# A decoder trunk on one Trainium2 core: the residual turned so that tokens lie on the partitions

## The chip, the core and the metric

The kernel runs on one core of a Trainium2 chip. The time is what the device takes for one execution, in microseconds, as the median of several runs. TensorE (PE, with its weight loads as PEld) multiplies; VectorE (DVE), ScalarE (ACT) and GpSimd (POOL) work element by element, and DMA queues issued by SyncE (SP) bring data in and out. On the chip, SBUF holds 128 partitions; products are summed in PSUM banks of 128 x 512 f32.

## What is computed

Two layers, each with a SwiGLU FFN, a mixer and a second FFN, on 512 tokens of width 1024. Each is wrapped in two RMS norms, over the 1024 features of a token:

```python
def _rmsnorm(x, g):
    return x * lax.rsqrt(jnp.mean(x * x, axis=-1, keepdims=True) + RMS_EPS) * g
def _swiglu(h, w_gate, w_up, w_down):            # 1024 -> 2816 -> 1024
    return (jax.nn.silu(h @ w_gate) * (h @ w_up)) @ w_down
...
for l in range(DEPTH):                            # 2 layers, g = norm_g[l]
    f = _swiglu(_rmsnorm(x, g[0]), ...)
    x = x + 0.5 * _rmsnorm(f, g[1])
    m = _mixer(_rmsnorm(x, g[2]), ...)
    x = x + _rmsnorm(m, g[3])
    f = _swiglu(_rmsnorm(x, g[4]), ...)
    x = x + 0.5 * _rmsnorm(f, g[5])
```

The mixer projects h into queries, keys and values of 8 heads of 64, a gated causal convolution of width 3 over 256 channels, and trailing means over 2, 4, 8 and 16 tokens with a small map over 256 more; the three results, 1024 channels, go through an output projection. The attention is a stick-breaking one: the weight of key s for query t is sigmoid(z) times the product of 1 - sigmoid(z) over the keys between them. The kernel takes that product as a sum of logarithms over the keys.

## The kernel before

**Precision.** Each f32 operand is split into a high part (a cast to f32r) and a low part (the rest). A product is three matmuls: high by high, high by low, low by high.

**Weights.** They come as units of 128 x 1024 (512 KB), each by one DMA. ACT makes the high part `wh` (L167), DVE the low part `wl` (L173). Raw units, parts and most larger tiles share a pool of 31 slots, and loads and splits run ahead as far as slots are free.

**The residual** `x` lies with features on the partitions: 8 blocks of 128 features by 512 tokens. A product's stationary operand is the weight, its moving operand 512 tokens of h.

**FFN.** The 22 blocks of 128 hidden channels come in chunks of 6, 8 and 8. For each block gate and up are accumulated over 8 blocks of features, in two PSUM banks `psz`. `evac` (L465 to L474) multiplies both by `rbs`, the broadcast norm factor, takes Silu on ACT, multiplies, and writes hid as high (ACT) and low part (POOL). After a chunk the down projection runs, one unit for each of the 8 feature blocks of the output, and DVE adds it to `f` (L512).

**Boundaries.** The last chunk's down projection (and likewise the mixer's output projection) is split: the last 7 units (5 for the mixer) run in token halves of 256 columns, so that the norm of the first half can start while PE works on the second. Squares are taken by ACT (L365) and summed over feature blocks by POOL and DVE into `ss` (L376). `rstd` sums `ss` over the partitions with one-column products (`pss<-mat,ss`), POOL takes the power -0.5 (L387), DVE puts the factors on a diagonal and PE broadcasts it over the partitions (`pss<-pH,none_`). `boundary` (L415 to L446) then multiplies f, adds to x, and makes the parts of h for two feature blocks at a time. h isn't normalised: the factor is applied where products leave PSUM.

**The order on PE** is that of the program: `mm` (L270) chains every matmul to the one ahead and adds to a running estimate of time. Side work (statistics, a head's sums and values) is a generator which names the delay after which it wants its next turn; `poll`, called between the products of a unit, starts what is due. `need` forces side work up to a flag.

**Attention.** A head's keys lie on the partitions and its queries along the free axis, in three tiles (384, 384 and 512 wide). `scores` makes logits and the logarithm `t` of 1 - sigmoid in parts `pH`, `pL` (L577, L581); `sums` adds the later keys inside a block by a triangular matrix `ntri` and those of later blocks by a matrix of minus ones, `none_`. Blocks needed together are added up first into a tile `later` by POOL (L622 to L624), which gets parts of its own. The projections of the next heads, the convolution and the pooling run between the heads' steps. Each eviction there multiplies by `rbs`; most additions of the pooling run on POOL.

## Time and profile before

| | us |
|---|---|
| median of 3 runs (2010.01 to 2014.77) | 2010.83 |
| the profiled execution | 2010.89 |
| its span on the core | 2009.1 |
| PE busy | 1928.6 (96%) |
| PE weight loads busy | 1658.7 (83%) |
| DVE busy | 1038.1 (52%) |
| ACT busy | 769.6 (38%) |
| POOL busy | 384.0 (19%) |

The profile is one execution, recorded by the hardware. Each instruction has a start, a length and, where it waited, the instruction that released it. Matmuls are pipelined, so the length of a single one is longer than its share of the time; the distance from start to start tells what it costs. A group of records written x2 is two in a row. The granted clock is the share of its full speed that TensorE got: 1.00 is 2.4 GHz, and a stretch partly at 1.2 GHz lies between .50 and 1.00. Stages of the first layer: first FFN to about 380 us, mixer to about 612, second FFN to about 1000; the second layer repeats them about 995 us later.

### The profile page before, as it was taken

Reading aid. Unit: us, or ns where it says so; the run is one execution under the profiler, and the core shown is the slowest. Engines: PE = TensorE matmul, PEld = TensorE weight load, DVE = VectorE, ACT = ScalarE, POOL = GpSimd, SP = SyncE. Lnnn points to the kernel's source line nnn. Section 1 sums busy time; section 2 is a strip of 40 time slices with the busy share of each in tenths; the row PEclk is TensorE's granted clock in tenths of the full one; section 3 lists DMA queues with packets and bytes.
Section 4 is the critical chain, followed back from the end, with each engine's and each line's share of the span. In section 5 each row is a group of like instructions: output and inputs, shape, how many; then the busy total and the mean of one; then the engine's idle time right before and its main releaser. Section 6 shows DMA issues by size and latency. Waiting matters only on the chain.

```text
span 2009.1 us, 25060 instructions
## 1 busy us (share of the span) xinstructions
PE 1928.6 (96%) x9908; PEld 1658.7 (83%) x9908; DVE 1038.1 (52%) x1487; ACT 769.6 (38%) x1223; POOL 384.0 (19%) x397
## 2 busy tenths in 40 slices
PE   8999999998989999999989999999998989999997
PEld 7888888887778888888988888888877888888887
DVE  7334434678857434434573343448687483343343
ACT  5223223456654332222443221335566442322232
POOL 3101011421315101001430010115131251010012
PEclk8999999999989999999999999999998989999998
DMA  5232323221221232232222323222211112323321
GB/s 198 78 124 74 115 92 108 74 63 43 65 72 43 84 126 84 85 115 89 93 72 94 105 84 115 86 93 74 65 62 53 63 63 75 125 84 97 113 74 43
DMA packets 52102, 174.19 MB, mean 87 GB/s; under 512 B 5520, under 2 KB 9872, under 8 KB 51984
## 3 DMA queue, kind: packets, MB, share of 16 engines
q1 hardware_dynamic: 51984, 172.59, 26.7%
q8 instruction: 78, 1.28, 0.3%
q14 instruction: 40, 0.33, 0.1%
HBM read 170.47 MB, written 2.10 MB: 86 GB/s over the span
## 4 chain that ended last, share of the span: by engine, by line
PE 83%; DVE 10%; ACT 3%; issue 2%; POOL 1%; DMA 0%; SPq 0%; DVEq 0%; ACTq 0%; POOLq 0%
PE psz L270 50%; PE psd L270 32%; DVE h L415 2%; DVE pH L439 2%; DVE pL L581 1%; DVE pH L577 1%; DVE wl L173 1%; PE pss L270 1%; ACT wh L167 1%; POOL x L442 1%; ACT h L414 1%; DVE t L614 1%; ACT t L347 0%; DVE ss L376 0%; ACT pL L365 0%
## 5 line engine op out<-in xcount | busy, mean ns | idle before, releaser
L270 PE MATMUL psz<-h,wh 128*128 128x512 f32 (+1 forms) x3168 | 906.6, 372 | 6.6 <-DVE t L465 3.0
L270 PEld LDWEIGHTS psz<-h,wh 128*128 128x128 f32 x3168 | 586.9, 194 | 105.0 <-issue 4.6
L270 PE MATMUL psz<-h,wl 128*128 128x512 f32 (+1 forms) x1584 | 587.3, 371 | 1.2 <-DVE wl L173 1.2
L173 DVE TENSOR_TENSOR wl<-raw,wh 128x1024 fp32r<-128x1024 f32 (+1 forms) x328 | 411.3, 1269 | 328.7 <-ACT wh L167 163.2
L270 PE MATMUL psd<-hid,wh 128*128 128x512 f32 (+1 forms) x1856 | 457.8, 338 | 0.0
L167 ACT CAST wh<-raw 128x1024 fp32r<-128x1024 f32 (+1 forms) x326 | 325.2, 1025 | 171.0 <-DVE wl L173 88.8
L270 PEld LDWEIGHTS psd<-hid,wh 128*128 128x128 f32 x1856 | 320.3, 190 | 37.7
L270 PEld LDWEIGHTS psz<-h,wl 128*128 128x128 f32 x1584 | 307.0, 194 | 49.3 <-DVE wl L173 1.7
L474 POOL TENSOR_TENSOR hid<-t,hid 128x512 fp32r<-128x512 f32 (+1 forms) x99 | 118.3, 1195 | 1112.1 <-ACT hid L473 1112.1
L270 PE MATMUL psd<-hid,wl 128*128 128x512 f32 (+1 forms) x928 | 313.9, 338 | 0.0
L466 DVE TENSOR_TENSOR t<-psz,rb 128x512 f32<-128x512 f32 (+1 forms) x99 | 62.4, 630 | 348.5 <-PE psz L270 348.5
L473 ACT CAST hid<-t 128x512 fp32r<-128x512 f32 (+1 forms) x99 | 56.6, 573 | 433.9 <-DVE t L468 433.8
L347 ACT ACTIVATE t<-t 128x512 f32<-128x512 f32 (+2 forms) x195 | 106.8, 571 | 247.1 <-DVE t L465 246.2
L270 PEld LDWEIGHTS psd<-hid,wl 128*128 128x128 f32 x928 | 176.2, 190 | 18.6
L270 PE MATMUL psd<-h,wh 128*128 128x512 f32 (+1 forms) x576 | 167.3, 377 | 0.0
L270 PEld LDWEIGHTS psd<-h,wh 128*128 128x128 f32 x576 | 106.3, 195 | 18.9 <-issue 1.0
L376 POOL TENSOR_TENSOR ss<-ss,pL 128x256 f32<-128x256 f32 x112 | 94.8, 851 | 101.4 <-ACT pL L365 96.9
L270 PE MATMUL psd<-h,wl 128*128 128x512 f32 (+1 forms) x288 | 107.3, 372 | 0.0
L465 DVE TENSOR_TENSOR t<-psz,rb 128x512 f32<-128x512 f32 (+1 forms) x99 | 61.7, 624 | 69.3 <-PE psz L270 68.7
L270 PE MATMUL psd<-mix,wh 128*128 128x256 f32 (+1 forms) x416 | 90.8, 317 | 0.1
L512 DVE TENSOR_TENSOR f<-f,psd 128x256 f32<-128x256 f32 (+1 forms) x92 | 47.6, 521 | 63.3 <-PE psd L270 63.3
L581 DVE TENSOR_TENSOR pL<-t,pH 128x384 fp32r<-128x384 f32 (+1 forms) x112 | 72.1, 664 | 12.2 <-ACT pH L579 9.9
(111 smaller groups left out, 1618.9 us busy)
## 6 DMA issues: line engine op xcount, KB each, us to landing
raw<-in_w_dram SPq DMA_DIRECT2D x296, 512.0 KB, 3.5
raw<-in_w_dram SPq DMA_DIRECT2D x32, 384.0 KB, 3.0
out_dram<-x SPq DMA_DIRECT2D x8, 256.0 KB, 2.8
x<-in_xt_dram SPq DMA_DIRECT2D x4, 256.0 KB, 5.5
x<-in_xt_dram SPq DMA_DIRECT2D x2, 512.0 KB, 9.3
mat<-in_mats_dram SPq DMA_DIRECT2D x1, 384.0 KB, 10.0
mat<-in_mats_dram SPq DMA_DIRECT2D x1, 128.0 KB, 8.5
cst<-in_consts_dram SPq DMA_DIRECT2D x1, 73.0 KB, 2.0
```

The costliest lines, as they stand in the source:

```text
L167: nc.scalar.copy(h[:, :n], raw[:, :n])
L173: nc.vector.tensor_tensor(lo[:, :n], raw[:, :n], f32(h[:, :n]), op=ALU.subtract)
L270: ins = nc.tensor.matmul(dst, w, r, start=start, stop=stop, skip_group_check=True)
L347: ins = nc.scalar.activation(out_, in_, f_, **kw)
L376: eng.tensor_tensor(ss[hf], ss[hf], qq, op=ALU.add)
L415: nc.vector.scalar_tensor_tensor(hL[k][:, ts], x[:, k, ts], g, f32(hH[k][:, ts]), op0=ALU.mult, op1=ALU.subtract)
L465: nc.vector.tensor_tensor(g[:, :n], pg[:, ts], rbs[:, ts], op=ALU.mult)
L466: nc.vector.tensor_tensor(u[:, :n], pu[:, ts], rbs[:, ts], op=ALU.mult)
L473: nc.scalar.copy(hid[0][:, ts], u[:, :n])
L474: nc.gpsimd.tensor_tensor(hid[1][:, ts], u[:, :n], f32(hid[0][:, ts]), op=ALU.subtract)
L512: nc.vector.tensor_tensor(f[:, n0, ts], f[:, n0, ts], ps[:, ts], op=ALU.add)
L581: eng.tensor_tensor(dstL, src, f32(dstH), op=ALU.subtract)
```

## The change

The residual is laid out as 4 blocks of 128 tokens by 1024 features.

- Down and output projections have the tokens of hid or of the mixer's result as the stationary operand (128 tokens) and the weights as the moving one (512 output features). A unit holds two blocks of input channels by half of the output features. The chunks are 8, 8 and 6. In the first two `stream` runs over both halves of the features with four banks; in the last, `by_tokens` finishes one token block after the other. The mixer's output projection has a part before the last head is done (`OUT_A`) and one behind it (`OUT_B`).
- Norms run along the free axis: ACT squares a block with a sum (`accum_out`), POOL takes the power of one column, DVE multiplies 1024 columns by factor and gain at once. Gains come as tiles of 128 x 1024 by DMA.
- h is normalised, then turned: 8 PE transposes of 128 x 128 in f32 for each token block into two banks, ACT casts the high part and DVE subtracts the low one. The turn is side work, due 13 us after the block's norm is issued. h has a place of its own, the pool has 28 slots, and `psz` has 5 banks in place of 4.
- `rbs`, the statistics and broadcast products, `later` and most of POOL's work are gone. Evictions read PSUM directly, the sums take more products with `none_`, and hid's low part and the pooling's additions are DVE's.
- At the start x comes block by block with an identity and the first gain, and h is made by the same norm and turn.

The core of the diff:

```diff
--- before.py
+++ after.py
-CHUNKS = (6, 8, 8)
+CHUNKS = (8, 8, 6)
...
-SLOTS = 31
+SLOTS = 28
...
+WARM = 24
+URGENT = 0
+
+OUT_A = ((4, 6), (7,))
+OUT_B = ((5, 0), (1, 2), (3,))
...
+D_TURN = 13
...
+                for dh in range(2):
+                    for g in _pairs(range(k0, k0 + n)):
+                        out.append(("down", l, half, (g, dh), len(g) * DH))
...
+    hHs = cpool.tile([P, KB, T], F32R, name="hh")
+    hLs = cpool.tile([P, KB, T], F32R, name="hl")
...
+        g = flat(kept("g", F32))
+        nc.sync.dma_start(out=g, in_=gains[l * 6 + i])
+        return g
...
+    def turn(dst, src):
+        ins = nc.tensor.transpose(dst, src, ident)
+        if line["last"] is not None:
+            after(ins, line["last"], "order")
+        line["last"] = ins
+        line["now"] += 0.1
...
+    def root(ms):
         nc.gpsimd.tensor_tensor(r, ms, expo, op=ALU.pow)
...
-        for i, v in enumerate((r, rest)):
-            for b in range(2):
-                nc.vector.tensor_scalar(dg[:, i, b * P:(b + 1) * P], ident, v[:, b:b + 1], -factor,
-                                        op0=ALU.mult, op1=ALU.mult)
-        yield D_BC if post else D_BC_PRE
-        ps = bank("s", 1)
-        for i in range(2):
-            mm(ps[:, :HALF], none_, dg[:, i, :], i == 0, i == 1)
-        return r, ps[:, :HALF]
...
+    def prenorm(key, tb, g, buf, free):
+
+        ss, ms = small(), small()
+        nc.scalar.activation(buf, x[:, tb, :], AF.Square, scale=D ** -0.5, accum_out=ss[:, 0:1])
+        nc.vector.tensor_scalar(ms[:, 0:1], ss[:, 0:1], EPS, None, op0=ALU.add)
+        r = root(ms[:, 0:1])
+        nc.vector.scalar_tensor_tensor(buf, x[:, tb, :], r, g, op0=ALU.mult, op1=ALU.mult)
+
+        def turned():
+            for q in range(2):
+                ps = bank()
+                for i in range(4):
+                    turn(ps[:, i * P:(i + 1) * P], buf[:, (4 * q + i) * P:(4 * q + i + 1) * P])
+                pv = ps.rearrange("p (a b) -> p a b", a=4)
+                dst = (slice(None), slice(4 * q, 4 * q + 4), tok(tb))
+                nc.scalar.copy(hHs[dst], pv)
+                nc.vector.tensor_tensor(hLs[dst], pv, f32(hHs[dst]), op=ALU.subtract)
+            done((key, "h", tb))
+            free()
+            return
+            yield
+
+        side(turned(), D_TURN)
...
+        def store(self, tb, dh, ps, f):
+
+            s = slice(dh * DH, (dh + 1) * DH)
+            if dh == 0:
+                self.ss[tb] = small()
+            nc.vector.tensor_tensor(f[:, s], f[:, s], ps, op=ALU.add)
+            nc.scalar.activation(tmp(), f[:, s], AF.Square, scale=self.scale,
+                                 accum_out=self.ss[tb][:, dh:dh + 1])
+            if dh == 1:
+                self.finish(tb, f)
+
+        def finish(self, tb, f):
+            ss, ms = self.ss.pop(tb), small()
+            nc.vector.scalar_tensor_tensor(ms[:, 0:1], ss[:, 0:1], self.eps, ss[:, 1:2], op0=ALU.add, op1=ALU.add)
+            r = root(ms[:, 0:1])
+            if self.pre is None:
+                for dh in range(2):
+                    s = slice(dh * DH, (dh + 1) * DH)
+                    nc.vector.scalar_tensor_tensor(f[:, s], f[:, s], r, self.post[:, s], op0=ALU.mult, op1=ALU.mult)
+                    nc.vector.tensor_tensor(x[:, tb, s], x[:, tb, s], f[:, s], op=ALU.add)
+                    nc.sync.dma_start(out=out[:, tb, s], in_=x[:, tb, s])
+                return
+            nc.vector.scalar_tensor_tensor(f, f, r, self.post, op0=ALU.mult, op1=ALU.mult)
+            nc.vector.tensor_tensor(x[:, tb, :], x[:, tb, :], f, op=ALU.add)
+            prenorm(self.key, tb, self.g, f, self.free)
...
+    def token_mms(ps, tb, src, blocks, w, dh_first, dh_last):
+        wH, wL = w
+        for i, b in enumerate(blocks):
+            poll()
+            sH, sL = src[b]
+            cs = slice(i * DH, (i + 1) * DH)
+            a, z = dh_first and i == 0, dh_last and i == len(blocks) - 1
+            mm(ps, sH[:, tok(tb)], wH[:, cs], a, False)
+            mm(ps, sH[:, tok(tb)], wL[:, cs], False, False)
+            mm(ps, sL[:, tok(tb)], wH[:, cs], False, z)
+
+    def stream(groups, src, store):
+
+        for dh in range(2):
+            pss = [bank("z") for _ in range(TBS)]
+            for gi, blocks in enumerate(groups):
+                w = take()
+                for tb in range(TBS):
+                    token_mms(pss[tb], tb, src, blocks, w, gi == 0, gi == len(groups) - 1)
+                    if gi == len(groups) - 1:
+                        store(tb, dh, pss[tb])
+                retire()
...
+    def by_tokens(groups, src, store):
+
+        ws = {}
+        for tb in range(TBS):
+            for dh in range(2):
+                ps = bank("z")
+                for gi, blocks in enumerate(groups):
+                    if tb == 0:
+                        ws[dh, gi] = take()
+                    token_mms(ps, tb, src, blocks, ws[dh, gi], gi == 0, gi == len(groups) - 1)
+                    if tb == TBS - 1:
+                        retire()
+                store(tb, dh, ps)
...
-            nc.vector.tensor_tensor(g[:, :n], pg[:, ts], rbs[:, ts], op=ALU.mult)
-            nc.vector.tensor_tensor(u[:, :n], pu[:, ts], rbs[:, ts], op=ALU.mult)
-            fn(g[:, :n], g[:, :n], AF.Silu)
-            nc.vector.tensor_tensor(u[:, :n], g[:, :n], u[:, :n], op=ALU.mult)
...
-            nc.scalar.copy(hid[0][:, ts], u[:, :n])
-            nc.gpsimd.tensor_tensor(hid[1][:, ts], u[:, :n], f32(hid[0][:, ts]), op=ALU.subtract)
...
+            fn(g, pg, AF.Silu)
+            nc.vector.tensor_tensor(u, g, pu, op=ALU.mult)
+            nc.scalar.copy(t[:, 0, :], u)
+            nc.vector.tensor_tensor(t[:, 1, :], u, f32(t[:, 0, :]), op=ALU.subtract)
+            return t[:, 0, :], t[:, 1, :]
...
+                    for tb in (2 * hf, 2 * hf + 1):
+                        need((n_, "h", tb))
...
-                            retire(2)
-                        when((key, "r", hf), lambda a=(pg, pu, HS[hf], hd): evac(*a))
...
-                project_out(f, hidH, hidL, n, store, finish, TAIL_F)
...
+                by_tokens(groups, src, lambda tb, dh, ps: bd.store(tb, dh, ps, f[tb]))
...
-            dense_out(range(KB), hidH, hidL, n, store)
...
+            stream(groups, src, store)
...
-                    s = tmp()
-                    eng = nc.gpsimd
-                    eng.tensor_copy(s[:, 256:384], ts[0][:, :P])
-                    eng.tensor_tensor(s[:, 384:], ts[0][:, P:256], ts[0][:, 256:384], op=ALU.add)
-                    eng.tensor_tensor(s[:, :256], s[:, 256:], t[:, P:384], op=ALU.add)
-                    self.later = self.parts(s, T, "later")
...
-                for to, src, c0, w in ((P, self.sp[0], 256, P),) if ti == 0 else (
-                        (P, self.later, 256, 256),) if ti == 1 else (
-                        (P, self.sp[1], 0, P), (256, self.later, 0, 256)):
-                    for part in src:
+                for to, src, c0, w in (((P, 0, 256, P),), ((P, 0, 0, 256), (256, 0, 256, P)),
+                                       ((P, 1, 0, 384), (256, 0, 0, 256), (384, 0, 256, P)))[ti]:
+                    for part in self.sp[src]:
                         mm(z[:, to:to + w], none_, part[:, c0:c0 + w], False, True)
...
-        def query_out(p, factor, ps):
-            t = tmp()
-            nc.vector.scalar_tensor_tensor(t, ps, factor, rbs, op0=ALU.mult, op1=ALU.mult)
...
+                    nc.scalar.activation(high[r, e, :], ps[r, :], AF.Identity, scale=factor)
...
-            nc.vector.tensor_tensor(t, ps, rbs, op=ALU.mult)
-            nc.gpsimd.tensor_tensor(u, u, t, op=ALU.mult)
+            nc.vector.tensor_tensor(u, u, ps, op=ALU.mult)
...
-                nc.gpsimd.tensor_tensor(s2[rows, w:], s[rows, w:], s[rows, :T - w], op=ALU.add)
...
+                nc.vector.tensor_tensor(s2[rows, 2 * w - 1:], s[rows, 2 * w - 1:], s[rows, w - 1:T + PAD - w], op=ALU.add)
...
-        project_out(f, [mix(i)[0] for i in blocks], [mix(i)[1] for i in blocks], KB, store, finish, TAIL_M,
-                    early=EARLY, flag=(key, "mix"))
...
+            s = slice(dh * DH, (dh + 1) * DH)
+            nc.scalar.copy(f[tb][:, s], ps)
...
+        by_halves(OUT_A, mixed, store)
...
+        need((key, "mix"))
...
+        bd = Boundary(key, l, i, pre)
+        by_tokens(OUT_B, mixed, lambda tb, dh, ps: bd.store(tb, dh, ps, f[tb]))
...
+    nc.sync.dma_start(out=x[:, 0, :], in_=xt[:, 0, :])
+    nc.sync.dma_start(out=ident, in_=mats[:, M_ID:M_ID + P])
+    slots["reserve"] += 1
+    g0 = gain(0, 0)
+    nc.sync.dma_start(out=x[:, 1, :], in_=xt[:, 1, :])
+    for i in range(2):
+        load(i)
+    for tb in range(2, TBS):
+        nc.sync.dma_start(out=x[:, tb, :], in_=xt[:, tb, :])
```

What moves on DVE is shown at three places. The first is the second head of the first mixer. Before, in the order of DVE (`t` is the logarithm, `later`'s parts are pH_3526 and pL_3527, tile 3's are pH_3539 and pL_3540, qk and q are the next query):

```order
L577 CAST pH_3526<-t_3522 128x512
L614 SCALAR_TENSOR_TENSOR t_3534<-psz_3530,t_3534 128x512
L719 SCALAR_TENSOR_TENSOR t_3582<-psd_3455,rb_226 128x512
L581 TENSOR_TENSOR pL_3527<-t_3522,pH_3526 128x512
L581 TENSOR_TENSOR mix_3567<-t_3564,mix_3567 64x512
L577 CAST pH_3539<-t_3534 128x512
L173 TENSOR_TENSOR wl_3577<-raw_3413,wh_3576 128x1024
L732 TENSOR_TENSOR qk_3584<-t_3582,q_3585 64x512
L581 TENSOR_TENSOR pL_3540<-t_3534,pH_3539 128x512
```

After, at the same head (the third tile is t_3140 with pH_3145 and pL_3146):

```order
L509 TENSOR_TENSOR pL_3120<-t_3114,pH_3119 128x384
L541 SCALAR_TENSOR_TENSOR t_3140<-psz_3136,t_3140 128x512
L506 CAST pH_3132<-t_3127 128x384
L586 TENSOR_TENSOR t_3170<-psz_3161,t_3170 64x512
L506 CAST pH_3145<-t_3140 128x512
L509 TENSOR_TENSOR pL_3133<-t_3127,pH_3132 128x384
L509 TENSOR_TENSOR pL_3146<-t_3140,pH_3145 128x512
L509 TENSOR_TENSOR mix_3173<-t_3170,mix_3173 64x512
L156 TENSOR_TENSOR wl_3183<-raw_2884,wh_3182 128x1024
```

The parts of `later`, the eviction with `rb`, a weight split and a query's part no longer stand between the third tile's logarithm and its low part.

The second place is the boundary behind the first mixer. Before, DVE multiplies f (`m`) by the broadcast factor, adds to x, and writes low parts of h for feature blocks:

```order
L439 TENSOR_TENSOR pH_5041<-m_4619,rbf_5038 128x512
L439 TENSOR_TENSOR pH_5077<-m_4619,rbf_5038 128x512
L439 TENSOR_TENSOR pH_5111<-m_4619,rbf_5038 128x512
L439 TENSOR_TENSOR pH_5156<-m_4619,rbf_5038 128x512
L442 TENSOR_TENSOR x<-x,pH_5156 128x2x256
L415 SCALAR_TENSOR_TENSOR h_5044<-x,cst,h_5044 128x256
L415 SCALAR_TENSOR_TENSOR h_5047<-x,cst,h_5047 128x256
L376 TENSOR_TENSOR ss_4646<-ss_4646,pL_5072 128x256
L415 SCALAR_TENSOR_TENSOR h_5080<-x,cst,h_5080 128x256
L415 SCALAR_TENSOR_TENSOR h_5083<-x,cst,h_5083 128x256
```

After, `f_4196`, `f_4208`, `f_4270` and `f_4294` are the four token blocks; L357 adds a half of the features, L374 and L375 are the norm behind and the residual, L321 the norm ahead, L331 the low part of turned h:

```order
L331 TENSOR_TENSOR hl<-psd_4529,hh 128x4x128
L331 TENSOR_TENSOR hl<-psd_4536,hh 128x4x128
L357 TENSOR_TENSOR f_4294<-f_4294,psz_4525 128x512
L156 TENSOR_TENSOR wl_4559<-raw_4362,wh_4558 128x1024
L374 SCALAR_TENSOR_TENSOR f_4270<-f_4270,ss_4514,g_4365 128x1024
L156 TENSOR_TENSOR wl_4568<-raw_4550,wh_4567 128x1024
L156 TENSOR_TENSOR wl_4585<-raw_4562,wh_4584 128x1024
L375 TENSOR_TENSOR x<-x,f_4270 128x1024
L357 TENSOR_TENSOR f_4294<-f_4294,psz_4577 128x512
L331 TENSOR_TENSOR hl<-psd_4602,hh 128x4x128
L331 TENSOR_TENSOR hl<-psd_4609,hh 128x4x128
```

The low part of block 1 (psd_4602) stands behind the last block's second addition, which needs the last product of the projection, and behind four weight splits, three of them shown.

The third place is the start. Before, DVE writes low parts of h for feature blocks (L415) as they come, with the first weight's split between them:

```order
L415 SCALAR_TENSOR_TENSOR h_104<-x,cst,h_104 128x256
L415 SCALAR_TENSOR_TENSOR h_107<-x,cst,h_107 128x256
L165 CAST wh_116<-raw_72 128x1024
L415 SCALAR_TENSOR_TENSOR h_110<-x,cst,h_110 128x256
L173 TENSOR_TENSOR wl_117<-raw_72,wh_116 128x1024
L415 SCALAR_TENSOR_TENSOR h_113<-x,cst,h_113 128x256
L415 SCALAR_TENSOR_TENSOR h_122<-x,cst,h_122 128x256
L415 SCALAR_TENSOR_TENSOR h_125<-x,cst,h_125 128x256
```

After, block 0's norm (f_119), two weight splits, then block 1's (ss_141, f_139):

```order
L319 TENSOR_SCALAR ss_121<-ss_120 128x1
L321 SCALAR_TENSOR_TENSOR f_119<-x,ss_124,g_108 128x1024
L156 TENSOR_TENSOR wl_128<-raw_111,wh_127 128x1024
L156 TENSOR_TENSOR wl_134<-raw_113,wh_133 128x1024
L319 TENSOR_SCALAR ss_141<-ss_140 128x1
L331 TENSOR_TENSOR hl<-psd_193,hh 128x4x128
L321 SCALAR_TENSOR_TENSOR f_139<-x,ss_144,g_108 128x1024
L331 TENSOR_TENSOR hl<-psd_200,hh 128x4x128
```

Both splits stand ahead of block 1's norm, and the first low parts of h behind block 0's turn.

## Rows read from the trace of the kernel before

**Rows 1.** stretches: length, busy us (count) of PE, PEld, DVE, ACT, POOL; clock, DMA, GB/s

```profile
0.00:50.00 50.00, 42.77 (x247) 37.23 (x248) 37.48 (x65) 25.87 (x44) 18.99 (x26) 0.86 0.55 198
50.00:360.00 310.00, 310.00 (x1439) 259.88 (x1439) 120.91 (x133) 91.23 (x119) 30.63 (x26) 1.00 0.30 96
372.00:420.00 48.00, 44.52 (x256) 39.02 (x255) 41.83 (x74) 24.00 (x46) 27.65 (x25) 0.93 0.23 77
420.00:587.00 167.00, 148.19 (x697) 124.05 (x697) 129.99 (x199) 107.98 (x188) 34.69 (x48) 0.92 0.20 64
612.00:662.00 50.00, 44.40 (x314) 43.49 (x313) 40.42 (x76) 23.39 (x49) 28.30 (x27) 0.86 0.16 53
...
996.00:1050.00 54.00, 48.97 (x368) 47.72 (x367) 47.19 (x87) 28.37 (x54) 26.93 (x25) 0.94 0.29 95
...
1984.00:2009.00 25.00, 13.24 (x103) 12.48 (x101) 13.37 (x27) 4.64 (x10) 8.04 (x7) 0.79 0.26 85
```

**Rows 2.** waits of PE, whole span: us in total, times, longest

```profile
PE pss L270 <- DVE ss L376: 21.8, 9, 3.0
PE psz L270 <- DVE pL L581: 21.5, 16, 1.8
PE psz L270 <- DVE pH L577: 10.6, 8, 3.9
```

**Rows 3.** groups by shape on PE: count, busy us, mean ns, idle before

```profile
L270 PE MATMUL psd<-hid,wh 128*128 128x256 f32 x896 | 162.0, 284 | 0.0
...
L270 PE MATMUL psd<-mix,wh 128*128 128x256 f32 x320 | 58.2, 284 | 0.1
...
L270 PE MATMUL pss<-mat,ss 128*128 128x1 f32 x96 | 16.5, 275 | 21.8 <-DVE ss L376 21.8
...
L270 PE MATMUL pss<-pH,none__80 128*128 128x256 f32 x48 | 11.2, 306 | 2.4 <-DVE rl L392 1.7 <-DVE rb L420 0.5 <-DVE pH L395 0.2
```

**Rows 4.** timeline of PE, first FFN's tail: start, length, operation, idle before

```profile
366.69 0.40 PE L270 MATMUL psd<-hid,wh 128*128 128x256 f32 x2
...
367.05 0.50 PE L270 MATMUL pss<-mat,ss 128*128 128x1 f32 x4
367.41 0.48 PE L270 MATMUL psd<-hid,wh 128*128 128x256 f32 x2
```

**Rows 5.** timeline of PE, a pooling map among projections

```profile
496.86 0.61 PE L270 MATMUL psd<-h,wh 128*128 128x512 f32 x2
...
497.54 1.02 PE L270 MATMUL psd<-c,mat 128*128 128x512 f32 x2
...
498.87 0.40 PE L270 MATMUL psd<-h,wl 128*128 128x512 f32 x1
```

**Rows 6.** timeline of DVE and PE, second head of the first mixer

```profile
451.19 0.67 DVE L581 TENSOR_TENSOR pL<-t,pH 128x512 fp32r<-128x512 f32 x1
...
452.73 1.20 DVE L173 TENSOR_TENSOR wl<-raw,wh 128x1024 fp32r<-128x1024 f32 x1
...
453.87 0.67 DVE L732 TENSOR_TENSOR qk<-t,q 64x512 fp32r<-64x512 f32 x1
...
454.47 0.67 DVE L581 TENSOR_TENSOR pL<-t,pH 128x512 fp32r<-128x512 f32 x1
...
455.19 0.50 PE L270 MATMUL psz<-pL,ntri 128*128 128x512 f32 x1 [1.84 <-DVE pL L581]
```

**Rows 7.** groups by shape on DVE and POOL

```profile
L173 DVE TENSOR_TENSOR wl<-raw,wh 128x1024 fp32r<-128x1024 f32 x296 | 375.1, 1283 | 297.7 <-ACT wh L167 144.6 <-PE psd L270 93.8 <-issue 57.9
...
L387 POOL TENSOR_TENSOR r<-ms,expo 128x2 f32<-128x2 f32 x24 | 28.5, 1187 | 81.3 <-DVE ms L385 75.4 <-DVE rl L392 5.9
...
L512 DVE TENSOR_TENSOR f<-f,psd 128x512 f32<-128x512 f32 x36 | 24.2, 680 | 0.0
```

**Rows 8.** timeline of PE: the first product on data, and the last product

```profile
7.53 0.48 PE L270 MATMUL psz<-h,wh 128*128 128x256 f32 x2 [1.59 <-ACT h L414]
...
1995.31 0.28 PE L270 MATMUL psd<-hid,wl 128*128 128x256 f32 x1
```

625 lines of the change are left out of this document (218 added, 407 removed).

## The prediction

> **What bounds the kernel now.** I read the busy times by stretch first. Between two stages TensorE works without a gap and at the full clock: 310.00 us busy of 310 at a granted clock of 1.00 [rows 1]. There the time is the number of products and nothing else, so a stretch that loses time shows as idle TensorE or as a lower clock. I take the loss of a stretch as its length less PE's busy time, plus its length times one less the clock. That gives 6.9 us for 372–420 (first FFN to mixer), 18.8 + 13.4 = 32.2 for the attention (420–587), 5.6 + 7.0 = 12.6 for mixer to second FFN (612–662), 5.0 + 3.2 = 8.3 for FFN to FFN (996–1050) and about 14 for the end [rows 1]. The second layer's stretches are the same within a microsecond. At the start 247 products of mostly 256 columns, about .12 us each (below), fill 30 of 50 us: 20 are lost. Two attentions, two boundaries before them, two behind them, one between layers, start and end: 146 us in all, seven parts in a hundred. The view of waits says for what: statistics products wait 21.8 us for DVE's sums of squares, and attention's sums wait 21.5 and 10.6 us for the low and high parts that DVE writes [rows 2]. So two things set the time: how many products there are, and how soon DVE gets to what PE wants next.
>
> **Products: the token halves.** The tails of the down and output projections run in token halves, 256 columns wide: 896 products with high weights of hid, hence 448 with low ones, and 320 + 160 of mix [rows 3]. Three of them take .36 us (366.69 to 367.05), .12 each [rows 4]; three of 512 columns take .68 (496.86 to 497.54), .227 each [rows 5]. A pair of halves so costs 13 ns more than one whole. Of the 1824 halves 912 pairs go; the projections of the first queries give another 96 and the wider head of the first FFN takes 48 back: 960 x 13.3 ns = **-12.8**. The 512-column products with tokens standing and weights moving are the same work as before otherwise, and I give them the same price.
>
> **Products: statistics.** 96 records of one column and 48 broadcasts of 256 go [rows 3]. Four of the first take .36 us (367.05 to 367.41), .09 each [rows 4]: 8.6; the second .12 each: 5.8. Together **-14.4**.
>
> **Products: `later`.** Without the pre-added sums every head needs two more products of 128 columns and two of 384. On the line through .12 for 256 and .227 for 512 these are .067 and .173: .48 a head, 16 heads, **+7.7**.
>
> **Products: transposes.** 192 blocks of 128 x 128 in f32 (six norms, four token blocks, eight each). No row shows one. The lower bound is a weight load with a one-column product, .09 [rows 4]. The upper one is an ordinary f32 product: between 497.54 and 498.87 lie one of 512 columns and two ordinary ones, 1.33 - .45 = .88 us, so .22 for 128 columns [rows 5]. I take .12, what a 256-column product costs, since it is near the lower row in form (one pass, a new weight each time): **+23**, bounds 17 to 42. All lie on PE's path, except where PE would have waited anyway. The Trainium skill, page TensorE: Matmul & The Clock Gate, Part 4: PE-mode transpose, speaks against the change here: about 275 ns for such a block inside a kernel, and the full clock not engaging for them. By that the transposes would be 53 us, and the sum 30 later. In this trace one-column products, each with a weight load of its own, come every 90 ns [rows 4], so I don't follow it.
>
> Products together: -12.8 - 14.4 + 7.7 + 23 = **+3.5**. PE's work is almost unchanged; the gain has to come from the waits.
>
> **Attention.** In the order of DVE the second head's last high part (453 us) is followed by a weight split, the query's low part and only then the low part that PE waits for: `pL` of `later` runs at 451.19, the split at 452.73, the query at 453.87, the wanted `pL` at 454.47, and PE starts at 455.19 after 1.84 us [rows 6]. The change takes from each mixer's DVE eight low parts of `later` (.67), eight evictions of queries and eight of convolution and pooling (.68): 16.3 us. It adds four multiplications and six pooling additions that POOL did, and two halves of subtractions: 12 x .68 = 8.2. So DVE, 130 us busy of 167 [rows 1], has 8 less, and nothing but the head's own work stands between its high and low parts. With these prices I followed DVE's queue head by head: waits of 1.7 at the second head, 3.5 at the third (pooling additions ahead of it), .8 at the fourth, 4 at the sixth (splits and convolution), 2 behind the last: 12 in place of 18.8. The half-clock loss falls with them, 13.4 to 8.6. That is -11.6 per mixer, **-23.2**; bounds 0 (the waits only move) and -23 per mixer (two thirds of the loss gone).
>
> **Boundaries.** Here the work changes its engine. For each token block DVE now does two additions to f (.68), three passes over 1024 columns (the price of a split, 1.28) and two low parts of h (.68): 6.6 us, with two powers on POOL (1.19 each) in between [rows 7]. Behind the mixer PE has 5 x 3 x 8 products = 27.2 us and 16 transposes to hide it. Up to the low part of block 1, which the first half of the next FFN needs, DVE's order holds 8 additions, 8 long passes, 4 splits, 4 low parts and 5 short ones (put at .16): 24.3 us, beginning 3.4 us into PE's run. If DVE waits for the first four norms, 2.2 us each (ACT's squares, power, hand-overs; an estimate from the power's 1.19), that is 36.5, while PE is through at 29.1: a wait of 7.4, which with some 5 us of lower clock is about the 12.6 of before: **0**, +-4 each. If the norms hide, only the last transposes, cast and subtraction are late, about 2.5. Behind an FFN PE has 6 x 3 x 8 products, 32.7 us: DVE at 36.5 against 34.6 leaves about 2 of wait with some 4 to 5 us of lower clock, 6.8 in place of 8.3 between layers, **-1.5**. Before the mixer the values take one block after another, 24 products (5.4 us) each; by the same queue PE waits about 3.5 at the third block, in place of a loss of 6.9 with its clock: **0**, +-3 each.
>
> **Start.** The first product on data stands at 7.53 us now [rows 8]. Afterwards two token blocks, an identity and a gain must land, and DVE has two weight splits queued ahead of block 1's norm, so PE begins at about 20, but then finds all it needs: 23 lost in place of 20, **+3** (-2 to +8). **End.** From the last product at 1995.31 [rows 8] to the end it takes 13.8 us: addition, squares, statistics, power, diagonals, broadcast, four multiplications, four additions, stores. Diagonals and broadcast go, and one block of 512 columns remains: addition, squares, power, two passes, a store: 9.5, **-4.3**.
>
> **Hidden.** The FFN's low part of hid moves from POOL to DVE, but two multiplications by the norm go there. DVE is busy 120.91 of 310 us [rows 1]; were this cover gone, every one of 88 hidden blocks would show up to .68 us. The gains add 6 MB of loads against a DMA share of .30 [rows 1].
>
> **Sum.** 3.5 - 23.2 - 1.5 + 3 - 4.3 = -22.5. The span of 2009.1 becomes 1986.6. The profiled run took 2010.89, 1.8 beyond its span, and the median of the runs is 2010.83: **1988 us**.
>
> **Rivals.** *More:* attention's waits and the lower clock almost vanish (-23 a mixer instead of -11.6) and the transposes cost .09 (-6): 1988 - 23 - 6 = 1959. For it: PE's waits there are all for DVE parts that stood behind others. Against: DVE stays over 70% busy there. *Nothing in attention:* the pooling additions and splits stand where `later` did, and PE waits as long: 1988 + 23 = 2011. For it: the splits are unchanged, ACT's chain of a head too. *Transposes as plain f32 products*, .22: +19, 2007; against it is the one-pass form, for it that every ordinary f32 product in the trace takes two records. (The Trainium skill's 275 ns would give 2018 for the same case.) *Slower:* DVE's chain of a boundary doesn't overlap with PE. Its place is the five boundaries; if each token block waits for the one ahead (addition to low part: 2 x .68 + 3 x 1.28 + 2 x .68 + 2 powers with hand-overs, about 11 us, four in a row 44) against 29 to 34 us of PE, each boundary loses 10 to 15 beyond its present loss: +50, 2038. It outweighs the gain from about 5 us per boundary on. Against it: the order interleaves two blocks.
>
> **How the numbers follow.** Forecast .57, with a range of its own of 1972 to 2003; more .12; nothing in attention .13; transposes .08; slower .10. A measurement here tells .3%, 6 us, from no change, so below 2004.8 is faster: the forecast less .02, all of the first rival, a quarter of the second and a third of the third: .73. Slower (above 2016.9): the last rival and a quarter of the second: .13. Between: .14. The range takes in half of the first rival, and leaves out most of the last: 1958 to 2022.
>
> **What would show it.** Right: transposes in rows of eight some .12 apart; PE busy for more than 153 of attention's 167 us, no wait of 2 us behind a split; the boundary behind the mixer with one wait of 2 to 7 us for DVE's h; a first product on data near 20 us; under 10 us behind the last. Wrong: transposes .2 or more apart; long PE waits for `f` or `hl` at each boundary; or weight splits that come late in the steady stretches, where PE has no idle time to hide them.

## The result

The changed kernel takes 1954.29 us (median of 4 runs, 1952.35 to 1954.8) against 2010.62 of the kernel before on the same chip: a ratio of 0.9714, with a 95% interval of 0.9697 to 0.9731. That is 56 us less, where 22.5 were forecast, and 4 us under the range of 1958 to 2022. The profiled execution took 1954.8 with a span of 1953.0.

| | before | after |
|---|---|---|
| span, us | 2009.1 | 1953.0 |
| PE busy | 96% | 98% |
| DVE busy, us | 1038.1 | 856.9 |
| POOL busy, us | 384.0 | 40.9 |

The stretches of the profile after, with the columns of [rows 1]: first the undisturbed part of the first FFN, then its boundary to the mixer, attention, the boundary to the second FFN, the one between the layers, and the second layer's attention.

```profile
58.00:357.00 299.00, 299.00 (x1295) 242.75 (x1294) 95.49 (x99) 82.45 (x101) 0.00 (x0) 1.00 0.28 95
357.00:418.00 61.00, 59.76 (x278) 49.05 (x277) 42.36 (x53) 27.39 (x47) 5.43 (x10) 1.00 0.30 102
418.00:566.00 148.00, 142.77 (x710) 119.50 (x708) 99.47 (x173) 98.30 (x183) 3.12 (x6) 1.00 0.12 42
566.00:650.00 84.00, 80.25 (x490) 72.51 (x490) 49.85 (x60) 38.12 (x63) 6.43 (x8) 0.94 0.37 132
...
972.00:1022.00 50.00, 48.93 (x369) 46.34 (x368) 32.47 (x40) 24.40 (x39) 4.72 (x5) 1.00 0.42 144
...
1382.00:1529.00 147.00, 142.65 (x706) 119.30 (x705) 99.59 (x173) 97.72 (x183) 3.33 (x7) 1.00 0.13 44
```

By the same measure as in the prediction, attention now loses 5.2 us, all of it idle time at a clock of 1.00, in place of 32.2 [rows 1]; the second layer's loses 4.4. The first of these ends at a lucky place: ahead of the last head's values PE waits 2.1 us, and the lower clock behind that wait begins where the stretch ends. The wait in the timeline of PE, and the four us behind the stretch:

```profile
564.16 0.50 PE L223 MATMUL psz<-pH,v 128*128 128x512 f32 x1 [2.12 <-ACT pH L508]
```

```profile
566.00:570.00 4.00, 4.00 (x13) 3.13 (x13) 1.61 (x2) 3.01 (x5) 0.00 (x0) 0.57 0.39 135
```

These 1.7 us belong to attention, which then loses 6.9: 25 less than before in the first layer and 28 less in the second, some 26.5 a mixer. The boundary ahead of the mixer loses 1.2 instead of 6.9, the one between layers 1.1 instead of 8.3, the one behind the mixer 3.8 idle and 5.0 by the clock, 8.8 instead of 12.6 (7.1 without those 1.7). The undisturbed stretch has PE busy for 299.00 of 299 us at 1.00, so DVE's new work is hidden there. The waits of PE over the whole span, which answer to [rows 2]:

```profile
PE psd L265 <- DVE f L321: 6.7, 3, 5.8
PE psz L223 <- DVE hl L331: 6.2, 2, 3.2
PE psz L223 <- DVE pL L509: 5.6, 10, 1.0
...
PE psz L223 <- ACT pH L508: 3.4, 2, 2.1
```

The three rows of [rows 2] summed to 54 us. The sums of a head now wait 5.6 us in all for their low parts, and the largest single wait, 5.8 us, is the one for block 1's norm at the start. The next rows are the timeline of PE, in order: the first product on data, eight transposes among the products of the first output projection and the products behind them, and the kernel's last product.

```profile
18.34 0.58 PE L223 MATMUL psz<-hh,wh 128*128 128x256 f32 x1
...
599.66 1.03 PE L265 MATMUL psd<-mat,f 128*128 128x128 f32 x8
600.45 0.48 PE L223 MATMUL psz<-wh,mix 128*128 128x512 f32 x1
600.76 0.39 PE L223 MATMUL psz<-wl,mix 128*128 128x512 f32 x1
601.00 0.62 PE L223 MATMUL psz<-wh,mix 128*128 128x512 f32 x2
...
1944.55 0.39 PE L223 MATMUL psz<-wh,hid 128*128 128x512 f32 x1
```

From the first of the eight transposes at 599.66 to the third product behind them at 601.00 it is 1.34 us. Two products are .45 of it, so a transpose costs .11. (The first product starts .79 us behind the first transpose, .099 for each, but then comes .31 ahead of the next one in place of .227.) The first product on data comes at 18.34 (forecast 20), and 8.45 us lie between the start of the last one and the end of the span (forecast 9.5, and 13.8 before).

One thing in the profile goes the other way. In the undisturbed stretches products that move 512 columns of h are further apart than before. The timeline of PE after, nine products from the first row to the last:

```profile
172.20 0.40 PE L223 MATMUL psz<-hh,wh 128*128 128x512 f32 x1
...
174.30 0.40 PE L223 MATMUL psz<-hh,wh 128*128 128x512 f32 x1
```

2.10 us for nine, .2333 each; in [rows 5] and in every steady stretch of before it is .227. Down products, which move weights, still come every .227.

### The profile page after: what moved, and what is told of

The parts are those of the page before. It is cut to its first block, busy times and chain, and to the rows that moved or that the text cites. A ratio compares the mean times of both kernels' runs of the same rounds, so it can differ in the third digit from the quotient of the medians.

```text
span 1953.0 us, 21947 instructions
## 1 busy us (share of the span) xinstructions
PE 1914.8 (98%) x9072; PEld 1588.2 (81%) x9072; DVE 856.9 (44%) x1090; ACT 714.0 (37%) x1089; POOL 40.9 (2%) x68
## 4 chain that ended last, share of the span: by engine, by line
PE 92%; DVE 4%; ACT 2%; DMA 1%; issue 1%; POOL 0%; SPq 0%; POOLq 0%; DVEq 0%; ACTq 0%
PE psz L223 80%; PE psd L223 11%; DMA raw<-in_w_dram 1%; DVE wl L156 1%; PE psd L265 1%; ACT t L296 0%; DVE hl L331 0%; DVE pL L509 0%; DVE f L321 0%; ACT t L538 0%; ACT pH L508 0%; POOL ss L312 0%; DVE t L541 0%; DVE x L375 0%; DVE f L357 0%
## 5 line engine op out<-in xcount | busy, mean ns | idle before, releaser
L223 PE MATMUL psz<-hl,wh 128*128 128x512 f32 (+1 forms) x1536 | 574.8, 374 | 7.2 <-DVE hl L331 6.2
L223 PE MATMUL psz<-hh,wh 128*128 128x512 f32 (+1 forms) x1536 | 575.0, 374 | 1.3 <-ACT hh L330 1.3
L223 PE MATMUL psz<-hh,wl 128*128 128x512 f32 (+1 forms) x1536 | 573.9, 374 | 0.0
L156 DVE TENSOR_TENSOR wl<-raw,wh 128x1024 fp32r<-128x1024 f32 x324 | 386.5, 1209 | 322.6 <-ACT wh L155 249.9
L223 PE MATMUL psz<-wh,hid 128*128 128x512 f32 x1408 | 437.3, 390 | 0.0
L155 ACT CAST wh<-raw 128x1024 fp32r<-128x1024 f32 x324 | 328.9, 1038 | 233.9 <-PE psz L223 177.5
L223 PEld LDWEIGHTS psz<-hl,wh 128*128 128x128 f32 x1536 | 292.2, 190 | 63.3 <-DVE hl L331 7.0
L223 PEld LDWEIGHTS psz<-hh,wh 128*128 128x128 f32 x1536 | 292.0, 190 | 57.4 <-ACT hh L330 2.4
L223 PEld LDWEIGHTS psz<-hh,wl 128*128 128x128 f32 x1536 | 292.1, 190 | 55.2
L223 PE MATMUL psz<-wl,hid 128*128 128x512 f32 x704 | 274.0, 389 | 0.0
L445 ACT CAST hid<-t 128x512 fp32r<-128x512 f32 x88 | 54.7, 622 | 462.4 <-DVE t L444 462.4
L223 PEld LDWEIGHTS psz<-wl,hid 128*128 128x128 f32 x704 | 132.2, 188 | 27.4
L223 PEld LDWEIGHTS psd<-hh,wl 128*128 128x128 f32 x320 | 60.2, 188 | 11.6
## 6 DMA issues: line engine op xcount, KB each, us to landing
mat<-in_mats_dram SPq DMA_DIRECT2D x1, 384.0 KB, 9.4
```

The costliest lines, as they stand in the source:

```text
L155: nc.scalar.copy(h[:, :n], raw[:, :n])
L156: nc.vector.tensor_tensor(lo[:, :n], raw[:, :n], f32(h[:, :n]), op=ALU.subtract)
L223: ins = nc.tensor.matmul(dst, w, r, start=start, stop=stop, skip_group_check=True)
L445: nc.scalar.copy(t[:, 0, :], u)
```

## Experiments

All times are medians, and each run stands beside runs of the kernel before on the same chip, which took between 2009.3 and 2010.9 us.

**h 32 bytes further on.** In the changed kernel hh and hl begin 32 bytes past a multiple of 64 in their partitions, behind a tile of constants of 200 bytes.

```diff
-    cst = cpool.tile([P, C_END], F32, name="cst")
+    cst = cpool.tile([P, 64], F32, name="cst")[:, :C_END]
...
-    expo = cpool.tile([P, 1], F32, name="expo")
+    expo = cpool.tile([P, 16], F32, name="expo")[:, 0:1]
```

> The changed kernel with h moved by 32 bytes: the tile of constants is padded, so that hh and hl begin at a multiple of 64 bytes in their partitions, as h does in the kernel before; nothing else changes. In the changed kernel a product that moves 512 columns of h comes every 233 ns in the undisturbed stretches, one that moves weights every 227. Theory address: all 4416 such products of the FFNs and projections go back to 227 ns, 4416 x 6.6 ns = 29 us less, 1925 us. Rival: it is h's place in one large tile, or the fifth PSUM bank, and the spacing stays at 233 ns: 1954 us.

1950.03 us (1947.78 to 1952.27). The spacing of the 512-column products stayed at 233 ns: alignment of h is not the cause. What moved is the 256-column products of the FFN's first units, most of them from 117 ns to 113. There are 1152, and at the full clock their mean falls by 4.0 ns: 4.6 us, about the whole difference of 4.3.

**The same, with weights 32 bytes off.** The second edit of the diff above is left out.

> As e1_aligned, with h aligned, but now weights, hid, mixer results and temporary tiles all begin 32 bytes past a multiple of 64. Theory that the moving operand's address counts: gate and up (h moves, weights stand) stay at 227 ns, down products (weights move, tokens stand) go to 233: 4 x 528 + 2 x 192 + 2 x 96 = 2688 products, +18 us against e1_aligned, 1943 us. Rival, the standing operand counts too: gate and up are slow as well, another 29 us, 1972 us. Rival, no address counts: the same as e1_aligned.

1953.64 us. Down products stay at 227 ns, products that move h at 233, and the halves are back at 117: neither theory's pattern. h aligned with weights off gives the same as h off with weights aligned. By the sizes of the tiles between them (the one of 4 bytes takes 32), h and the slots are 32 bytes off a multiple of 2048 from each other in both kernels, and 64 bytes in e1_aligned. So if addresses count, it is the distance between a product's two operands.

**The distance set to zero.** The lines that allocate hh and hl move behind the other constants, next to the slots, so that both addresses leave the same remainder modulo 4096.

```diff
-    hHs = cpool.tile([P, KB, T], F32R, name="hh")
-    hLs = cpool.tile([P, KB, T], F32R, name="hl")
...
     expo = cpool.tile([P, 16], F32, name="expo")[:, 0:1]
+    hHs = cpool.tile([P, KB, T], F32R, name="hh")
+    hLs = cpool.tile([P, KB, T], F32R, name="hl")
```

> As e1_aligned, with hh and hl allocated last ahead of the pool of slots, so that the address of h and that of every slot leave the same remainder modulo 4096, as in the kernel before, where h lay in slots itself. Theory, the place of the moving operand relative to the standing one counts: products that move h come every 227 ns again in place of 233, 4416 of them, 29 us less than e1_aligned, 1921 us; values (h stands, weights move) fall from 235 to 227 ns too. Rival, it is h's own stride or its large tile: no change, 1950 us.

1926.91 us (1925.9 to 1928.44): 23.1 less than e1_aligned, 27.4 less than the changed kernel, and a ratio of 0.9583 (0.9566 to 0.96) to the kernel before. The same nine products in its timeline:

```profile
172.17 0.39 PE L223 MATMUL psz<-hh,wh 128*128 128x512 f32 x1
...
174.21 0.39 PE L223 MATMUL psz<-hh,wh 128*128 128x512 f32 x1
```

2.04 us, .2267 each. 4416 products give back 29.1 us and the values some .4, while the 1152 halves go from 114.3 ns on average to 119.9 and take 6.5: 23.0, as measured. This version is faster than both kernels.

**Other distances.** 2048 bytes (the constant `expo` ahead of hh, the four small matrices behind hl) and 64 (`expo` behind hl):

```diff
+    expo = cpool.tile([P, 16], F32, name="expo")[:, 0:1]
     hHs = cpool.tile([P, KB, T], F32R, name="hh")
     hLs = cpool.tile([P, KB, T], F32R, name="hl")
```

> As v0_same_place, with h 2048 bytes off the slots' remainder modulo 4096. If the remainder modulo 2048 or less is what counts, products that move h come every 227 ns as in v0_same_place, about 1921 us; if modulo 4096, they stay at 233, about 1950 us. Under the rival (h's tile itself) 233 in both.

> As v0_same_place, with h 64 bytes off the slots' remainder modulo 4096. If any offset between the two operands costs the extra 6.6 ns, the spacing is 233 ns and the time about 1950 us; if the remainder modulo 64 is what counts, it is 227 and about 1921 us.

One execution each: 1927.57 us with a spacing of 227 ns at 2048, 1951.88 with 233 at 64. So 2048 bytes more cost nothing, and 64 off cost the same as 32 off (the changed kernel). These are distances between tiles. Inside a unit the standing operand begins at every multiple of 512 bytes in its slot, and all 24 products of a unit come every 226 to 227 ns in v0_same_place: a distance of any multiple of 512 is as good as none. Other distances, between 64 and 512 say, were not tried.

**Every transpose twice.**

```diff
                 for i in range(4):
                     turn(ps[:, i * P:(i + 1) * P], buf[:, (4 * q + i) * P:(4 * q + i + 1) * P])
+                    turn(ps[:, i * P:(i + 1) * P], buf[:, (4 * q + i) * P:(4 * q + i + 1) * P])
```

> As e1_aligned, with every transpose issued twice (the second writes the same result), 192 more. Theory: a transpose costs .099 us of PE's path, as its spacing in the trace says: +19 us against e1_aligned, about 1944 us. Rival of the prediction, they cost the price of an ordinary f32 product (.22): +42 us. Rival, half of them fall into waits for DVE's h and cost nothing there: +10 us. If they draw the clock down behind them, more than 19.

1969.43 us, 19.4 more than e1_aligned: .101 for each of 192. Transposes lie on PE's path at about the price that the timeline shows, and the clock stays up (a granted 1.00 from 560 to 650, where e1_aligned has .98).

**`later` put back into the changed kernel,** on e1_aligned, with its lines in `scores` and `sums`:

```diff
...
+                    eng.tensor_tensor(s[:, :256], s[:, 256:], t[:, P:384], op=ALU.add)
+                    self.later = self.parts(s, T, "later")
...
+                        (P, self.later, 256, 256),) if ti == 1 else (
+                        (P, self.sp[1], 0, P), (256, self.later, 0, 256)):
```

> As e1_aligned, with one part of the change undone: the pre-added tile later is back (three POOL operations a head, a cast and a low part on DVE, and two products with none_ fewer per part). PE has 7.7 us less to do. Theory: DVE's parts of later, and POOL's additions beside DVE, bring attention's waits back in part, 5 to 10 us a mixer: about 1925 - 8 + 15 = 1932 us. Rival: later had no share in the waits, the relief comes from the evictions and from POOL's other work: 1917 us. If later was the whole cause, 27 us a mixer come back: 1970 us.

1960.06 us, 10 more, although PE has 7.7 less to do. Attention's stretch in e1_aligned and then in e4_later:

```profile
415.00:570.00 155.00, 150.37 (x735) 125.85 (x734) 103.84 (x178) 103.08 (x191) 4.17 (x8) 0.99 0.15 50
```

```profile
415.00:570.00 155.00, 145.47 (x681) 119.56 (x680) 109.89 (x183) 105.05 (x194) 18.52 (x32) 0.96 0.13 43
```

Idle time and clock lose 4.6 + 1.6 in the first and 9.5 + 6.2 in the second: 9.5 us a mixer.

**`later` taken out of the kernel before,** the same part of the change alone:

```diff
...
-                    self.later = self.parts(s, T, "later")
...
+                for to, src, c0, w in (((P, 0, 256, P),), ((P, 0, 0, 256), (256, 0, 256, P)),
+                                       ((P, 1, 0, 384), (256, 0, 0, 256), (384, 0, 256, P)))[ti]:
```

> The kernel before with one part of the change alone: later and its POOL additions and parts are gone, the sums take more products with none_ (7.7 us of PE). From the reverse (e4_later, 10 us with later back): about 2010 - 10 = 2000 us. If later was all that slowed attention, 27 us a mixer less: 1965 us. If the rest of POOL's and DVE's work there keeps the waits, the products come on top: 2015 us.

1979.2 us (1976.39 to 1981.58): 31 less, with 7.7 us more of products. This one part does more than half of what the whole change did. Attention's stretch in its trace:

```profile
420.00:575.00 155.00, 145.43 (x726) 124.91 (x725) 116.06 (x183) 106.64 (x188) 19.23 (x24) 0.96 0.22 70
```

9.6 us idle and 6.2 by the clock: 15.8 in place of 32.2 [rows 1]. So `later` cost 16.4 us a mixer, where the prediction counted .67 a head, 5.4 a mixer, for its low part.

**POOL beside DVE.** Why so much? Of the casts of parts on DVE in the trace of before, 24 of those with 512 columns ran with POOL idle and took 413 ns on average, the other 8 ran mostly beside POOL's work and took 1088. Of those with 384 columns 30 of 32 ran mostly beside POOL and took 709; in the changed kernel 30 ran with POOL idle and took 353. In e7_before_no_later POOL still does the pooling, and its trace shows one such place. The timeline of DVE, POOL and PE:

```profile
503.59 1.03 POOL L771 TENSOR_TENSOR t<-t 128x508 f32<-128x508 f32 x1
503.78 1.73 DVE L577 CAST pH<-t 128x384 fp32r<-128x384 f32 x2
504.68 0.62 POOL L769 COPY t<-t 64x512 f32<-64x512 f32 x1
...
505.44 1.21 DVE L173 TENSOR_TENSOR wl<-raw,wh 128x1024 fp32r<-128x1024 f32 x1
505.53 2.23 POOL L771 TENSOR_TENSOR t<-t 64x504 f32<-64x504 f32 x1
506.57 1.47 DVE L577 CAST pH<-t 128x512 fp32r<-128x512 f32 x1
507.96 1.61 DVE L581 TENSOR_TENSOR pL<-t,pH 128x384 fp32r<-128x384 f32 x3
...
508.56 0.69 PE L270 MATMUL psz<-pL,ntri 128*128 128x384 f32 x1 [3.23 <-DVE pL L581]
```

The two casts of 384 columns take 1.73 us together beside POOL, then come a weight split and the cast of 512 columns with 1.47 us, and only then the low part for which PE waits 3.23 us. In the changed kernel a cast of 512 columns takes .41 and one of 384 .36. Two runs measure POOL's part by itself. In the first, POOL's three operations of `later` are back in e1_aligned, and nobody uses them:

```diff
...
+                    eng.tensor_copy(s[:, 256:384], ts[0][:, :P])
+                    eng.tensor_tensor(s[:, 384:], ts[0][:, P:256], ts[0][:, 256:384], op=ALU.add)
+                    eng.tensor_tensor(s[:, :256], s[:, 256:], t[:, P:384], op=ALU.add)
```

> As e1_aligned, with POOL's three operations of later in each head back, and nothing that uses them: no cast, no low part, the same products on PE. It measures POOL's work beside DVE by itself. Theory: DVE's casts and low parts, which read and write SBUF only, run up to twice as long while POOL works (in the kernel before the cast of a part took 413 ns with POOL idle and 789 with POOL busy), 1 to 3 us a head, of which some reaches PE: 3 to 8 us a mixer, 1956 to 1966 us. Rival: e4_later's 10 us come from the two extra operations on DVE's queue, and POOL beside it costs nothing: 1950 us.

1966.57 us, 16.5 more than e1_aligned, 8 a mixer. e4_later, with the cast and the low part besides, is 10.0 us slower than e1_aligned at 7.7 us less of products, 17.7 in all; so by difference POOL's three operations are nearly the whole price of `later` there, and DVE's own two about 1 us. In the second POOL works on tiles of its own, on v0_same_place:

```diff
...
+                    eng.tensor_copy(own_[:, 0:1], ts[0][:, 0:1])
+                    eng.tensor_copy(own_[:, 0:1], t[:, 0:1])
+                    eng.tensor_copy(own_[:, :P], mat[:, :P])
+                    eng.tensor_tensor(own_[:, :P], mat[:, P:2 * P], mat[:, 2 * P:3 * P], op=ALU.add)
+                    eng.tensor_tensor(own_, own_, mat[:, P:3 * P], op=ALU.add)
```

> On v0_same_place: as e5_pool_beside, but POOL's three operations of each head work on tiles of their own and only start when the head's tiles are there (two one-column copies wait for them), so that no temporary tile is held longer. The same columns, the same places, nothing that uses the results. Theory, POOL's accesses slow DVE's: most of e5's 16 us come back, 1927 + 8 to 16 = 1935 to 1943 us. Rival, e5's cost came from the temporary tiles that POOL held: 1927 us.

1935.97 us, 9.1 more than v0_same_place. Work on POOL that takes two single columns from a head and gives nothing back costs 4.5 us a mixer, though POOL is busy 2.3 us a head with it and 1.8 in e5_pool_beside. The other 7 of the 16.5 us there fit the temporary tiles that POOL held, by difference only. The casts of 384 columns on DVE, by shape, in the kernel before, in the changed one (with those of 512) and in e5c:

```profile
L577 DVE CAST pH<-t 128x384 fp32r<-128x384 f32 x32 | 21.3, 687 | 0.1
```

```profile
L506 DVE CAST pH<-t 128x384 fp32r<-128x384 f32 x32 | 11.6, 361 | 0.3
...
L506 DVE CAST pH<-t 128x512 fp32r<-128x512 f32 x16 | 6.6, 414 | 0.0
```

```profile
L508 DVE CAST pH<-t 128x384 fp32r<-128x384 f32 x32 | 15.5, 484 | 0.3
```

687 ns on average before, 361 after, 484 with POOL's idle work: it is the same instruction. The Trainium skill, page SBUF — State Buffer, section SBUF: two separate sides, says why: DVE in a two-port mode or with two inputs from SBUF and POOL hold one pair of ports in turn, each for its whole instruction. The traces agree: above, POOL's addition at 505.53 starts behind the split and takes 2.23 us in place of 1.03, longer by the split's 1.21, and the cast at 506.57 then ends only after it. DVE's operations that read PSUM kept their length (678 ns mostly beside POOL and 675 without for the logarithm's last step of 512 columns, in the kernel before).

**What the rest is not.** Attention's loss falls by some 26.5 us a mixer; `later` explains 16.4. Five runs looked for the rest, the first on v0_same_place with four banks for psz in place of five, and four for psd in place of three:

```diff
-        return ppool.tile([P, 512], F32, tag=tag, bufs=5 if tag == "z" else 3, name=uid("ps" + tag))
+        return ppool.tile([P, 512], F32, tag=tag, bufs=4, name=uid("ps" + tag))
...
```

> On v0_same_place: psz has four PSUM banks in place of five and psd four in place of three, so that attention's logits have as many banks as in the kernel before. Theory: the fifth bank has little share in attention's gain, 1927 us within 4. Rival: with four banks a head's logits wait for evictions again, 5 to 10 us a mixer, 1937 to 1947 us.

1926.98 us: the fifth bank has no share. Then queries and keys out of PSUM by way of DVE:

```diff
-                    nc.scalar.activation(high[r, e, :], ps[r, :], AF.Identity, scale=factor)
+                t = tmp()
+                nc.vector.tensor_scalar(t, ps, factor, None, op0=ALU.mult)
...
+                    nc.scalar.copy(high[r, e, :], t[r, :])
```

> On v0_same_place: queries and keys leave PSUM through a DVE multiplication into a temporary tile, as in the kernel before, and their parts are made from that: eight more DVE operations of 512 columns a mixer. Theory, DVE's queue counts: 5.5 us of DVE more a mixer, of which a third to a half reaches PE, 2 to 3 us a mixer, 1931 to 1933 us. Rival, DVE has room where these stand: 1927 us.

1926.79 us: eight evictions by DVE a mixer cost nothing here. Then POOL's work for pooling and convolution (additions, copies and multiplications) goes to DVE in the kernel before without `later`, and the pooling's additions go from DVE to POOL in v0_same_place:

```diff
-                nc.gpsimd.tensor_tensor(s2[rows, w:], s[rows, w:], s[rows, :T - w], op=ALU.add)
+                nc.vector.tensor_tensor(s2[rows, w:], s[rows, w:], s[rows, :T - w], op=ALU.add)
...
```

```diff
-                nc.vector.tensor_tensor(s2[rows, 2 * w - 1:], s[rows, 2 * w - 1:], s[rows, w - 1:T + PAD - w], op=ALU.add)
+                nc.gpsimd.tensor_tensor(s2[rows, 2 * w - 1:], s[rows, 2 * w - 1:], s[rows, w - 1:T + PAD - w], op=ALU.add)
```

> On e7_before_no_later (the kernel before without later, 1979 us): the pooling's additions and copies and the convolution's multiplications run on DVE in place of POOL, so that POOL has only memsets in attention. Attention still loses some 10 us more than in the changed kernel's mixer. Theory, POOL beside DVE is the rest too: 4 to 7 us a mixer, 1965 to 1971 us. Rival, the rest is DVE's own queue, which gets longer by 16 to 18 operations of up to .7 us a mixer: 1979 to 1985 us.

> On v0_same_place (1927 us): the reverse, the pooling's six additions a mixer run on POOL in place of DVE. Theory, POOL beside DVE costs more than the 4 us of DVE's time that it takes over: 1928 to 1935 us. Rival, DVE's queue counts more: 1922 to 1926 us.

1978.44 and 1928.61 us, less than 2 us from their bases of 1979.2 and 1926.91. What POOL takes from DVE by working beside it and what DVE has to do instead are about equal for the pooling. Last, more weight splits:

```diff
-        nc.vector.tensor_tensor(lo[:, :n], raw[:, :n], f32(h[:, :n]), op=ALU.subtract)
+        for _ in range(2 if st.get("mixing") else 1):
+            nc.vector.tensor_tensor(lo[:, :n], raw[:, :n], f32(h[:, :n]), op=ALU.subtract)
...
```

> On v0_same_place (1927 us): while attention runs, the low part of each weight unit is computed twice by DVE, 16 operations more a mixer, about 18 us of DVE among the heads' own work. In the kernel before, 21 weight splits lay in attention's stretch, in the changed one 12. Theory, the splits between a head's operations are what is left of attention's gain: 18 us of them cost 5 to 10 us a mixer, 1937 to 1947 us. Rival, they fall into DVE's idle time: 1927 to 1930 us.

1932.31 us (1928.85 to 1933.48), 5.4 more: 16 splits cost 2.7 us a mixer, so the 9 that left attention's stretch explain about 1.5. The remaining 8 to 9 us a mixer stay open; these runs show no cause for them. One candidate was not tried: the pooling's tiles, which are five of their own in the changed kernel and before come from the seven temporary tiles that the logarithms use too.

## Why the prediction was wrong

- **Attention, -11.6 a mixer: about -26.5 measured.** This is the step that failed. The place was right (DVE's queue between a head's high and low parts), and so was the way of the change; the term was mis-sized. I added up lengths of DVE operations that go and come, each at the mean of its rows, and left POOL out, whose work in attention was 34.69 us [rows 1]. `later` stood in that sum with 5.4 us a mixer for its low parts; taken out alone it gave 16.4 (e7_before_no_later). I forgot its casts, and I gave no price to POOL's three operations, which cost 8 us a mixer on e1_aligned with nothing that uses them (e5_pool_beside), and like work on tiles of its own 4.5 (e5c_pool_own). DVE's busy time in the stretch fell from 129.99 [rows 1] to 99.47, not by 8. Its rows there, before and then after:

```profile
L173 DVE TENSOR_TENSOR wl<-raw,wh 128x1024 fp32r<-128x1024 f32 x21 | 25.8, 1242 | 3.4 <-ACT wh L167 3.4
L581 DVE TENSOR_TENSOR pL<-t,pH 128x384 fp32r<-128x384 f32 x32 | 19.9, 639 | 2.3 <-ACT pH L579 1.8 <-PE psz L270 0.5
...
L577 DVE CAST pH<-t 128x512 fp32r<-128x512 f32 x16 | 9.2, 582 | 0.0
```

```profile
L509 DVE TENSOR_TENSOR pL<-t,pH 128x384 fp32r<-128x384 f32 x32 | 17.5, 552 | 3.8 <-ACT pH L508 3.6
L156 DVE TENSOR_TENSOR wl<-raw,wh 128x1024 fp32r<-128x1024 f32 x12 | 14.6, 1219 | 1.6 <-ACT wh L155 1.6
...
L506 DVE CAST pH<-t 128x512 fp32r<-128x512 f32 x8 | 3.3, 414 | 0.0
```

Of these 30 us some 10 are weight splits that now run outside the stretch, 8 are those that I counted, 5 the casts of `later`, and some 8 the shorter casts and low parts of the other tiles: the time that POOL took from DVE, which the means held. And where I walked the queue with longer operations I let waits of 12 us remain, with a clock loss of 8.6; measured are 4.4 to 5.2 us idle and at most 1.7 by the clock. For 8 to 9 us of the gain a mixer no run shows the cause. The rival *more* came nearest (-23), at .12; that its time of 1959 lies so close to the measured one is luck, since +27 in products, which it did not have, and -26 at the boundaries, where it had -1.5, cancel.
- **Products, +3.5.** Transposes cost .11 instead of .12, 21 us instead of 23 (e3_turn_twice: 19.4), so the counted products come to +1.7. The 275 ns of the Trainium skill's page TensorE: Matmul & The Clock Gate, Part 4: PE-mode transpose, stand there beside a figure for bf16 blocks and don't hold for these f32 blocks in a row: the measurement is 110.
- **Same price for the same product: failed.** I wrote that the other 512-column products keep their price. Those that move h went from 226.7 to 233.3 ns, 27.4 us in all with the values and halves (v0_same_place), because the new place of h is 32 bytes off a multiple of 512 from the slots. Nothing in the prediction looked at where tiles lie. Without it the forecast would have missed by 61 us, not by 34.
- **Boundaries, 0, 0 and -1.5: -5.7 (-4.2 in the second layer), -3.8 (-5.5) and -7.2.** The norms' chain was shorter than I put it. I took the power at 1.19 [rows 7]; after it takes .55 in most places of the timeline, and DVE's passes no longer run beside much POOL work. Low parts of h in the kernel before took 888 ns mostly beside POOL and 474 without, multiplications of f 1412 and 686. Behind the mixer PE waits 3.0 us where I expected 7.4. How much of it is POOL and how much the order was not tried.
- **Start and end.** By the products that either stretch holds the start is +4, and +2 where its transposes and statistics are left to their own terms (forecast +3). The end is -5.3 (forecast -4.3). The loss there before I put at about 14; by the measure that I named it is 17 (11.8 idle and 5.3 by the clock, [rows 1]), on which no term rests.
- **Sum.** +1.7 + 27.4 for products, -54.7 for attention to the borders of its stretches, -9.9, -9.3 and -7.2 for boundaries, +2 and -5.3: about -55, against -56.1 in the spans.

## What to carry to other kernels

A mean duration taken from a trace holds what ran beside it: before pricing DVE's operations, split their rows, shape by shape, by whether POOL was busy, and don't take POOL's work as free. When operands move to another tile, compare the addresses of a product's standing and moving operand with those of before; a spacing read in one steady stretch shows it at once. And when one part of a large change can be done alone, as `later` here, its own rows deserve a price of their own, with its effect on every engine.

## What the runs showed of the hardware

An f32r product that moves 512 columns takes 226.7 ns when its two operands lie a multiple of 512 bytes apart in their partitions (v0_same_place, v2048), and 233.3 when they lie 32 bytes (the changed kernel, e2_weights_off) or 64 bytes (e1_aligned, v64) off that. For 256 columns it is the other way round: 120 ns at a multiple of 512, 117 at 32 bytes off, and at 64 off 113 in some stretches and 118 in others. Why, no run here tells. An f32 transpose of 128 x 128, eight or sixteen in a row among f32r products, costs 110 ns. A DVE cast of 512 columns from f32 to f32r took 413 ns with POOL idle and 1088 on average beside POOL's work in SBUF (the kernel before).
